# Stores of a feed-forward stage through GpSimd's transfer queue, and the next column's raw weight tiles requested at a column's start

## The chip, the core and the metric

The kernel runs on one core of a Trainium2 chip. Its engines are TensorE (PE, with weight loads shown as PEld), VectorE (DVE), ScalarE (ACT), GpSimd (POOL) and SyncE (SP, which only issues transfers here). Each engine works through its own list of instructions in the order in which the built program has them, and waits on semaphores where it needs another's result. The metric is the device time of one execution in microseconds.

## The reference

Two layers of a bidirectional encoder. Each has a mixer (gated linear attention in layer 0, spatial gating in layer 1) and a SwiGLU feed-forward block, with normalisations and conditioning around them. What the change touches lies in the feed-forward block, which occurs once in each layer:

```
a, bb = jnp.split(h @ ffn_w_in[i], 2, axis=-1)
y = (jax.nn.silu(a) * bb) @ ffn_w_out[i]
x = x + g2 * rms_norm(y, norm_g[i, 3])
```

`h` has 1024 features. There are 1024 tokens of one request, and 256 of another; the same weights serve both. `ffn_w_in` is 1024 x 5632 (2816 hidden features for `a`, 2816 for `bb`), `ffn_w_out` is 2816 x 1024. All in 32-bit floats.

## The kernel before

**Numbers.** A float32 operand is split into two parts that TensorE takes at full rate: a rounded high part (a cast on ACT, line 145) and the rest (a subtraction on DVE, line 146). Each product is then three matmuls: high by high, high by low, low by high.

**Token blocks.** The 1024 tokens are two blocks, A and B, of 512; the 256 tokens of the other request are block C.

**First feed-forward product, `ffn_in`.** It goes over 22 columns of 128 hidden features. The first two are done plainly. The other 20 (the loop `for j in range(NPL, NH)`) take blocks A and B together with the seven products of a Strassen-like scheme, so that four combinations of a column's weights are needed: `ua`, `us`, `ub`, `ut`. `ua` and `ub` are the raw weight tiles of the `a` half and the `bb` half, 128 x 1024 each (called A-tile and B-tile in the prediction). `us` and `ut` are made from both by four DVE operations (`sums`, lines 173 to 176: first the sum of the B-tile's halves, last the A-tile overwritten in place). Each of the four is split on ACT and DVE (lines 145, 146). The raw tiles come from a pool of three buffers (`rawp`). The loads are issued on SP by `raw` (lines 131, 134).

In the loop, one PSUM bank `a` collects several products in a row. It is read by DVE between them: line 1337 adds it to `c22`, and only when that has read it may TensorE start the next group, `seven(a, wb, 1, T[4], False)`. Line 1348 reads it once more for `gb`. Line 1341 finishes block C's column, which line 1264 (`store_c`) stores to `gdr`.

**Beside the columns.** Two generators run between the column's groups, by a credit that `tick` gives:

- `rights` (lines 1211 to 1231): for every two columns, it builds seven combinations of the products and stores them to `tdr`, 256 KB each (line 1213).
- `lefts` (lines 1234 to 1249): it prepares combinations of `ffn_w_out` for the second product. It works in 22 pieces for each layer. A piece loads two 256 KB halves into one buffer `y` (line 1240), does four DVE operations (lines 1242, 1243, 1245, 1246) in place, and stores 512 KB to `sdr` (line 1248). There is one buffer, so that the next piece's loads wait for the store to land.

**What sets the order.** The code is written in the order of the above, but the framework's scheduler orders each engine's instructions itself, by its own estimates. In the built program all 22 pieces of a layer stand in the first ten or eleven columns, two or three to a column; in an even column they stand otherwise than in an odd one. All transfers go through SP's queue, in the order that SP has them: an SP entry that waits holds up those behind it. GpSimd has 42 entries in the whole program, none of them within a layer's 20 columns.

Of the kernel before, what the change touches and what calls it, by code (L numbers as in the profile page):

```python
# [38 lines left out]
def encoder_kernel(  # L39
# [7 lines left out]
    nc = tc.nc  # L47
    pe, act, dve, pool, dma = nc.tensor, nc.scalar, nc.vector, nc.gpsimd, nc.sync.dma_start

    const = ctx.enter_context(tc.tile_pool(name="const", bufs=1))  # L50
    hp = ctx.enter_context(tc.tile_pool(name="hp", bufs=1))
    rawp = ctx.enter_context(tc.tile_pool(name="rawp", bufs=3))
# [6 lines left out]
    def nm(s):  # L59
        uid[0] += 1  # L60
        return f"{s}_{uid[0]}"
# [9 lines left out]
    def ps_ax():  # L71
        return psp.tile([128, 512], F32, tag="ax", bufs=3, name=nm("pax"))

    def ps_so():
        return psp.tile([128, 512], F32, tag="so", bufs=3, name=nm("pso"))
# [22 lines left out]
    src = {"A": (x_sample[0], 0), "B": (x_sample[0], 512), "C": (x_prompt[0], 0)}  # L98
# [15 lines left out]
    g_dr = [drp.tile([128, NH, 256], F32, name=nm("gdr")) for _ in range(2)]  # L114
    t_dr = [{o: drp.tile([128, NK, 512], F32, name=nm("tdr" + o)) for o in RUNS} for _ in range(2)]
    s_dr = [drp.tile([128, NK, 4, 512], F32, name=nm("sdr")) for _ in range(2)]


    class Units:
        def __init__(self):  # L120
            self.specs = []
            self.ready = []
            self.pos = 0
            self.n = 0
            self.spare = None
            self.pair = None

        def raw(self, src, shape):
            raw = rawp.tile([128, 1024], F32, tag="raw", name=nm("raw"))
# [19 lines left out]
        def load(self):  # L149
            key, src, shape = self.specs[self.pos]  # L150
            self.pos += 1
            n = 1024
            if key[0] == "ua":
                self.pair = [self.raw(x, 128) for x in src]
                w = self.pair[0]
            elif key[0] == "us":
                w = self.sums()
            elif key[0] == "ub":
                w = self.pair[1]
            elif key[0] == "ut":  # L160
                w = self.pair[0]
            else:
                w = self.raw(src, shape)
                if shape is not None:
                    n = src.shape[1] * src.shape[2]
            self.ready.append((key, *self.parts(w, key[0][0] == "u", n)))

        def sums(self):
            a, b = self.pair
            s = self.sum_tile()  # L170
            a1, a2, b1, b2 = a[:, 0:512], a[:, 512:1024], b[:, 0:512], b[:, 512:1024]
            s1, s2 = s[:, 0, :], s[:, 1, :]
            dve.tensor_add(s1, b1, b2)  # L173
            dve.tensor_sub(s2, s1, a1)
            dve.tensor_sub(a1, a1, b1)
            dve.tensor_sub(a2, a2, s2)
            return s.rearrange("p s c -> p (s c)")
# [5 lines left out]
        def next(self, key, ahead=2):  # L183
            self.ahead(1)
            k, hi, lo = self.ready.pop(0)
            assert k == key, (k, key)
            self.ahead(ahead)
            return hi, lo

    units = Units()  # L190
# [991 lines left out]
    def ffn_in(L, gens_in, fp, t_in):  # L1182
        td = t_dr[L]
# [26 lines left out]

        def rights(k, a, b, c, d):
            def put(o, t):
                dma(out=td[o][:, k, :], in_=t)

            yield 3.0
            for o, t in (("1", a), ("2", c), ("3", d)):
                put(o, t)
            x = bt.tile([128, 512], F32, tag="r", name=nm("x"))
            dve.tensor_sub(x, b, a)
            yield 1.4  # L1220
            dve.tensor_sub(b, d, b)
            yield 1.4
            put("5", x)
            dve.tensor_add(a, b, a)
            yield 1.4
            put("7", b)
            dve.tensor_sub(c, a, c)
            yield 1.4
            put("6", a)
            yield 1.4  # L1230
            put("4", c)


        def lefts():
            w = ffn_w_out[L].rearrange("(k t p) (h c) -> k p t h c", t=2, p=128, h=2)
            for k in range(NK):
                for c0 in (0, 256):
                    t = both[:, 2:4, :].rearrange("p i (u c) -> p (i u) c", u=2)
                    for i in range(2):
                        dma(out=t[:, 2 * i : 2 * i + 2, :], in_=w[k][:, i, :, c0 : c0 + 256])  # L1240
                    yield 12.0
                    dve.tensor_add(t[:, 3, :], t[:, 1, :], t[:, 3, :])
                    dve.tensor_sub(t[:, 1, :], t[:, 0, :], t[:, 1, :])
                    yield 1.0
                    dve.tensor_sub(t[:, 0, :], t[:, 3, :], t[:, 0, :])
                    dve.tensor_sub(t[:, 2, :], t[:, 2, :], t[:, 0, :])
                    yield 6.0
                    dma(out=s_dr[L][:, k, :, c0 : c0 + 256], in_=t)
                    yield 1.0

        def x_part(blk, h):
            return tuple(t[blk][:, 4 * h : 4 * h + 4, :] for t in (hhi, hlo))

        def seven(ps, w, half, x, start):
            hi, lo = w
            xh, xl = x
            for k in range(4):
                c = slice((4 * half + k) * 128, (4 * half + k + 1) * 128)
                for l, r in ((hi, xh), (hi, xl), (lo, xh)):
                    pe.matmul(ps, lhsT=l[:, c], rhs=r[:, k, :], start=start, stop=(k == 3 and l is lo), skip_group_check=True)  # L1260
                    start = False

        def store_c(j, s):
            dma(out=g_dr[L][:, j, :], in_=s)

        def plain(blk, j, w, part, s):
            n = BLK[blk]
# [12 lines left out]
        ua, ub = [], []  # L1280
        for ib, blk in enumerate(ORDER):
# [4 lines left out]
            for j in range(NPL):  # L1286
# [3 lines left out]
                if blk == "C":  # L1290
                    s = bt.tile([128, 256], F32, tag="accC", bufs=1, name=nm("gc"))
                else:
                    s = place[blk][:, j, :]
# [7 lines left out]
        both = ypart("A", 1)  # L1301
        units.sum_tile = lambda: both[:, 0:2, :]
        fill.push(lefts())
        for j in range(NPL, NH):
            last = j == NH - 1
            wa, ws, wb, wt = [units.next((u, L, j), 0) for u in ("ua", "us", "ub", "ut")]
            a, c = ps_so(), ps_ax()
            t1 = bt.tile([128, 512], F32, tag="t", name=nm("c11"))
            u2 = bt.tile([128, 512], F32, tag="r", name=nm("u2"))
            seven(a, wa, 0, x_part("B", 0), True)  # L1310
            act.copy(t1, a)
            tick(2.7, 0.7)
            seven(c, wa, 1, x_part("B", 1), True)
            dve.tensor_add(t1, t1, c)
            act.activation(t1, t1, AF.Silu)
            tick(2.7, 0.7)
            units.ahead(2)
            pc = ps_ax()[:, :256]
            mm3(pc, wa, "C")
            sc = bt.tile([128, 256], F32, tag="xk", bufs=3, name=nm("sc"))  # L1320
            act.activation(sc, pc, AF.Silu)
            tick(2.9, 0.7)
            seven(a, ws, 1, T[2], False)
            act.copy(u2, a)
            tick(2.7, 0.7)
            b = psp.tile([128, 512], F32, tag="mm", bufs=2, name=nm("pmm"))
            seven(b, ws, 0, x_part("A", 0), True)
            c22 = bt.tile([128, 512], F32, tag="sq", name=nm("c22"))
            act.copy(c22, b)
            tick(2.7, 0.7)  # L1330
            if not last:
                units.ahead(3)
            else:
                t_in(2, 2)
            vec.drain()
            seven(a, wt, 0, T[3], False)
            dve.tensor_add(c22, c22, a)  # L1337
            tick(2.7, 0.7)
            pc = ps_ax()[:, :256]
            mm3(pc, wb, "C")  # L1340
            dve.tensor_mul(sc, sc, pc)
            store_c(j, sc)
            tick(2.9, 0.7)
            if not last:
                units.ahead(4)
            seven(a, wb, 1, T[4], False)
            gb = t1 if j % 2 else bt.tile([128, 512], F32, tag="accB", bufs=1, name=nm("gb"))
            dve.tensor_mul(gb, t1, a)
            tick(2.7, 0.7)
            seven(b, wt, 1, x_part("A", 1), False)  # L1350
            t2 = bt.tile([128, 512], F32, tag="xk", bufs=3, name=nm("c12"))
            dve.tensor_add(t2, u2, b)
            act.activation(t2, t2, AF.Silu)
            ga = t2 if j % 2 else bt.tile([128, 512], F32, tag="accA", bufs=1, name=nm("ga"))
            dve.tensor_mul(ga, t2, c22)
            if j % 2:
                vec.push(rights(j // 2, *even, ga, gb))
            else:
                even = ga, gb
            tick(2.7, 0.7)  # L1360
# [378 lines left out]
```

## Time and profile before

| | |
|---|---|
| median of 3 runs | 2790.35 us (2790.24 to 2792.02) |
| the profiled execution's own time | 2790.62 us |
| its span, first to last instruction | 2788.9 us |
| mean granted TensorE clock | 0.991 |
| PE busy | 2714.6 us, 97% of the span |
| DVE busy | 1774.4 us, 64% |
| ACT busy | 1117.3 us, 40% |
| POOL busy | 36.1 us, 1% |
| transfers | 410.41 MB, all issued on SP but for instructions; engines of the queue busy 44.9% |

How to read it: PE is the engine to keep busy, and 74 us of the span it is not. The questions are where these lie, and what ended each. A row of the view of waits names the engine that waited, with the tile and line of its instruction, then what ended the wait, then the total in us, the number of waits, and the longest. A row of the timeline gives the start and the duration in us, the engine (with q for its sequencer), the line, the operation and the tiles, written first; in brackets stands the idle time before it. In these rows `y` is the buffer of `lefts` and also other tiles, `c` is `c11`, `c12` or `c22`, and `raw<-in_ffn_w_in_dram` is a raw weight tile.

Line 1337, once in each of the 20 columns, runs from 776.4 to 1262.6 us of the span in layer 0, and from 2003.5 to 2496.1 us in layer 1.

### The profile page before, as it was taken

The numbers are of one execution on the slowest core, as the hardware profiler recorded it, in microseconds if no ns is written. First come the engines' busy times: TensorE is split into PE (matmuls) and PEld (weight loads), VectorE is DVE, ScalarE is ACT, GpSimd is POOL, SyncE is SP. The second block draws the span as 40 slices with busy tenths as digits, with TensorE's granted clock in tenths as the row PEclk, the third lists the DMA queues.
The fourth block names the chain that finished last, engine by engine and source line by source line (L and its number), as shares of the span: only waits on it lengthen the run. The fifth ranks groups of instructions, "written<-read, shape, count | busy, mean of one in ns | idle before, by whom it ended". The sixth has DMA issues, their size and how long they took to land.

```text
span 2788.9 us, 36997 instructions
## 1 busy us (share of the span) xinstructions
PE 2714.6 (97%) x14164; PEld 2279.1 (82%) x14164; DVE 1774.4 (64%) x2781; ACT 1117.3 (40%) x1892; POOL 36.1 (1%) x48
## 2 busy tenths in 40 slices
PE   7999999999999999999999999999999999999998
PEld 4887888977888788888778888878878888888886
DVE  6762746587865654447778587676855644447576
ACT  5442434454632223324357354426422223234443
POOL 0001000000000000000000000000000000000000
PEclk9999999999999999999999999999999999999999
DMA  6224232156255542237777312454255532238676
GB/s 232 69 67 144 80 108 71 52 170 188 95 168 166 188 137 77 96 97 261 265 244 242 125 39 93 153 158 148 94 167 177 176 99 89 74 125 296 209 238 210
DMA packets 317542, 410.41 MB, mean 147 GB/s; under 512 B 21058, under 2 KB 194820, under 8 KB 317364
## 3 DMA queue, kind: packets, MB, share of 16 engines
q1 hardware_dynamic: 317364, 408.04, 44.9%
q8 instruction: 111, 1.82, 0.3%
q14 instruction: 67, 0.55, 0.1%
HBM read 304.65 MB, written 103.32 MB: 146 GB/s over the span
## 4 chain that ended last, share of the span: by engine, by line
PE 70%; DVE 12%; DMA 12%; issue 2%; ACT 2%; SPq 1%; POOL 0%; DVEq 0%; ACTq 0%; POOLq 0%
PE pso L1260 11%; PE pmm L1260 5%; PE pmm L322 4%; DMA y<-in_ffn_w_out_dram 3%; PE pax L1260 3%; PE pmm L309 2%; PE pmm L308 2%; PE pmm L307 2%; PE pax L307 2%; PE pax L308 2%; PE pso L1433 2%; PE pax L309 2%; PE pso L1434 2%; PE pso L1435 2%; DVE ulo L146 2%
## 5 line engine op out<-in xcount | busy, mean ns | idle before, releaser
L145 ACT CAST uhi<-raw 128x1024 fp32r<-128x1024 f32 (+1 forms) x299 | 307.2, 1030 | 648.7 <-issue 285.3
L146 DVE TENSOR_TENSOR ulo<-raw,uhi 128x1024 fp32r<-128x1024 f32 (+1 forms) x299 | 358.5, 1201 | 215.9 <-ACT uhi L145 214.6
L309 PE MATMUL pax<-hhiC,ulo 128*128 128x256 f32 x680 | 192.6, 283 | 0.0
L307 PE MATMUL pax<-hhiC,uhi 128*128 128x256 f32 x680 | 192.5, 283 | 0.0
L308 PE MATMUL pax<-hloC,uhi 128*128 128x256 f32 x680 | 192.4, 283 | 0.0
L1260 PE MATMUL pso<-t,uhi 128*128 128x512 f32 x428 | 149.8, 412 | 24.1 <-DVE c L1337 24.1
L1433 PE MATMUL pso<-uhi,hhiB 128*128 128x512 f32 x374 | 146.0, 391 | 0.9 <-DVE y L1416 0.5
L1434 PE MATMUL pso<-uhi,hloB 128*128 128x512 f32 x374 | 145.6, 389 | 0.0
L1435 PE MATMUL pso<-ulo,hhiB 128*128 128x512 f32 x374 | 145.6, 389 | 0.0
L307 PEld LDWEIGHTS pax<-hhiC,uhi 128*128 128x128 f32 x680 | 130.3, 192 | 3.8 <-ACT v L580 0.4
L308 PEld LDWEIGHTS pax<-hloC,uhi 128*128 128x128 f32 x680 | 130.2, 191 | 3.1
L309 PEld LDWEIGHTS pax<-hhiC,ulo 128*128 128x128 f32 x680 | 130.2, 191 | 1.7 <-issue 1.7
L371 DVE SCALAR_TENSOR_TENSOR aacc<-wada,sct,aacc 128x1024 f32<-128x1024 f32 x98 | 122.1, 1279 | 13.4 <-DMA wada<-in_w_ada_dram 13.3
L1382 ACT CAST hhiB<-tl 128x512 fp32r<-128x512 f32 x154 | 94.6, 619 | 89.1 <-DMA tl<-tdr 33.2
L1383 DVE TENSOR_TENSOR hloB<-tl,hhiB 128x512 fp32r<-128x512 f32 x154 | 106.0, 701 | 34.1 <-ACT hhiB L1382 34.0
L1260 PEld LDWEIGHTS pso<-t,uhi 128*128 128x128 f32 x428 | 81.4, 197 | 42.5 <-DVE c L1337 26.3
L1260 PE MATMUL pso<-y,uhi 128*128 128x512 f32 x324 | 109.2, 391 | 0.0
L173 DVE TENSOR_TENSOR y<-raw 128x512 f32<-128x512 f32 x40 | 27.6, 691 | 109.1 <-DMA raw<-in_ffn_w_in_dram 109.1
L1433 PE MATMUL pmm<-uhi,hhiB 128*128 128x512 f32 x242 | 94.7, 391 | 0.3 <-ACT y L1403 0.3
L1434 PE MATMUL pmm<-uhi,hloB 128*128 128x512 f32 x242 | 94.2, 389 | 0.0
L1435 PE MATMUL pmm<-ulo,hhiB 128*128 128x512 f32 x242 | 94.2, 389 | 0.0
L1433 PEld LDWEIGHTS pso<-uhi,hhiB 128*128 128x128 f32 x374 | 70.2, 188 | 18.6 <-DVE y L1416 1.4
(470 smaller groups left out, 7296.8 us busy)
## 6 DMA issues: line engine op xcount, KB each, us to landing
wada<-in_w_ada_dram SPq DMA_DIRECT2D x96, 512.0 KB
raw<-in_ffn_w_in_dram SPq DMA_DIRECT2D x88, 512.0 KB
tl<-tdr SPq DMA_DIRECT2D x154, 256.0 KB
raw<-in_ffn_w_out_dram SPq DMA_DIRECT2D x74, 512.0 KB
y<-in_ffn_w_out_dram SPq DMA_DIRECT2D x88, 256.0 KB
sdr<-y SPq DMA_DIRECT2D x44, 512.0 KB
raw<-sdr SPq DMA_DIRECT2D x40, 512.0 KB
tdr<-c SPq DMA_DIRECT2D x60, 256.0 KB
```

The costliest lines, as they stand in the source:

```text
L145: act.copy(hi[:, :n], raw[:, :n])
L146: dve.tensor_sub(lo[:, :n], raw[:, :n], hi[:, :n].bitcast(F32))
L307: pe.matmul(ps, lhsT=hi[:, c], rhs=hhi[blk][:, k, :], start=(k == 0), stop=False)
L308: pe.matmul(ps, lhsT=hi[:, c], rhs=hlo[blk][:, k, :], start=False, stop=False)
L309: pe.matmul(ps, lhsT=lo[:, c], rhs=hhi[blk][:, k, :], start=False, stop=(k == KD - 1))
L322: pe.matmul(ps, lhsT=l, rhs=r, start=(i == 0), stop=(i == 3 * KD - 1))
L371: dve.scalar_tensor_tensor(out=a, in0=ring[k % 2], scalar=sc, in1=a, op0=ALU.mult, op1=ALU.add)
L1260: pe.matmul(ps, lhsT=l[:, c], rhs=r[:, k, :], start=start, stop=(k == 3 and l is lo), skip_group_check=True)
L1383: dve.tensor_sub(lo, t, hi.bitcast(F32))
L1433: pe.matmul(ps, lhsT=th[:, t], rhs=hi[:, c], start=(k == 0), stop=False)
L1434: pe.matmul(ps, lhsT=tl[:, t], rhs=hi[:, c], start=False, stop=False)
L1435: pe.matmul(ps, lhsT=th[:, t], rhs=lo[:, c], start=False, stop=(k == NK - 1))
```

## The change

The three kinds of stores of `ffn_in` (to `tdr`, `sdr` and `gdr`) are issued by GpSimd and no longer by SP: 154 stores to `tdr`, 44 to `sdr` and 44 to `gdr`. And the raw tiles of the next column are requested when a column begins, by a method of their own, instead of with the next `ua`.

```diff
+    store = pool.dma_start
...
-                self.pair = [self.raw(x, 128) for x in src]
+                if self.coming is None:
+                    self.pairs_ahead()
+                self.pair, self.coming = self.coming, None
                 w = self.pair[0]
...
+        def pairs_ahead(self):
+            if self.coming is None:
+                key, src, shape = next((x for x in self.specs[self.pos - 1 :] if x[0][0] == "ua"), (None, None, None))
+                if key is not None:
+                    self.coming = [self.raw(x, 128) for x in src]
...
             def put(o, t):
-                dma(out=td[o][:, k, :], in_=t)
+                store(out=td[o][:, k, :], in_=t)
...
-                    dma(out=s_dr[L][:, k, :, c0 : c0 + 256], in_=t)
+                    store(out=s_dr[L][:, k, :, c0 : c0 + 256], in_=t)
...
         def store_c(j, s):
-            dma(out=g_dr[L][:, j, :], in_=s)
+            store(out=g_dr[L][:, j, :], in_=s)
...
             wa, ws, wb, wt = [units.next((u, L, j), 0) for u in ("ua", "us", "ub", "ut")]
+            if not last:
+                units.pairs_ahead()
```

What it does to the order of instructions: TensorE's order is the same, and DVE's and ACT's differ by exchanges of neighbours. SP's list is shorter by the stores, and GpSimd's is longer by them. In the changed kernel the line numbers are 1 to 11 higher.

On SP, in layer 0, within one odd column of the time when `lefts` runs. `y` is the buffer of `lefts`, `raw` with a number a raw weight tile (8436 is a B-tile, 8628 the A-tile of the column after). Before:

```order
L1240 DMA y_6838<-in_ffn_w_out_dram 128x2x256 x2
L1213 DMA tdr_36_123<-ga_8203 128x512
L1248 DMA sdr_137<-y_6838 128x4x256
L1240 DMA y_6838<-in_ffn_w_out_dram 128x2x256
L134 DMA raw_8436<-in_ffn_w_in_dram 128x8x128
L1213 DMA tdr_41_128<-x_8414 128x512
L1240 DMA y_6838<-in_ffn_w_out_dram 128x2x256
L134 DMA raw_8628<-in_ffn_w_in_dram 128x8x128
L1248 DMA sdr_137<-y_6838 128x4x256
L1264 DMA gdr_121<-sc_8281 128x256
```

After, the same place (8396 is that B-tile, 8597 that A-tile):

```order
L1249 DMA y_6838<-in_ffn_w_out_dram 128x2x256 x4
L135 DMA raw_8396<-in_ffn_w_in_dram 128x8x128
L1249 DMA y_6838<-in_ffn_w_out_dram 128x2x256 x2
L135 DMA raw_8597<-in_ffn_w_in_dram 128x8x128
L1249 DMA y_6838<-in_ffn_w_out_dram 128x2x256 x4
```

The stores are gone from between the loads. The B-tile's load now stands ahead of both `y` loads of its piece, where it stood between them; the A-tile's load stands behind them as it did.

On GpSimd, which had nothing there before, the same stretch now reads (the first five rows belong to the odd column, the rest to the even column after it):

```order
L1257 DMA sdr_137<-y_6838 128x4x256
L1222 DMA tdr_36_123<-ga_8203 128x512
L1257 DMA sdr_137<-y_6838 128x4x256
L1222 DMA tdr_41_128<-x_8418 128x512
L1257 DMA sdr_137<-y_6838 128x4x256
L1273 DMA gdr_121<-sc_8281 128x256
L1222 DMA tdr_42_129<-c_1380_8213 128x512
L1222 DMA tdr_38_125<-gb_8186 128x512
L1222 DMA tdr_37_124<-ga_8203 128x512
L1222 DMA tdr_40_127<-c_1394_8390 128x512
L1257 DMA sdr_137<-y_6838 128x4x256
```

All stores of a layer are now one list of their own, in the order in which DVE finishes their data. Four stores to `tdr` and one to `gdr` stand ahead of the last store to `sdr` in this piece.

More of the change, by code (lines that the diff above doesn't have):

```diff
@@ L125, in __init__ @@
             self.spare = None
-            self.pair = None
+            self.pair = self.coming = None
         def raw(self, src, shape):
```

## The prediction

> **What bounds the kernel now.** I read the page first, then the waits of TensorE, then three stretches of equal work side by side, then the timelines of VectorE and SyncE in the stretch that loses time.
>
> ```profile
> PE 2714.6 (97%) x14164; PEld 2279.1 (82%) x14164; DVE 1774.4 (64%) x2781; ACT 1117.3 (40%) x1892; POOL 36.1 (1%) x48
> PE pso L1260 <- DVE c L1337: 24.1, 11, 4.6
> ```
>
> TensorE is the bound, and GpSimd is free. The largest wait of TensorE in the whole program, 24.1 us in 11 places, is for line 1337, in the stage that the change touches. The next view gives the columns from one line 1337 to another: eight of layer 0 and nine of layer 1, with the pieces of `lefts` in them, and two later ones, with no pieces left. (Columns: length, then busy time of PE, PEld, DVE, ACT, POOL, then granted clock, DMA share, GB/s.)
>
> ```profile
> 776.36:989.27 212.91, 203.51 (x1056) 174.49 (x1055) 127.75 (x209) 58.36 (x80) 0.00 (x0) 0.98 0.54 176
> 2003.46:2246.96 243.50, 229.59 (x1193) 196.63 (x1191) 142.04 (x231) 65.39 (x90) 0.00 (x0) 0.99 0.52 169
> 1088.47:1138.19 49.72, 49.72 (x265) 42.91 (x264) 24.31 (x34) 14.84 (x20) 0.00 (x0) 1.00 0.26 85
> ```
>
> A free column takes 49.72 / 2 = 24.86 us. Eight take 198.9, so layer 0 loses 14.0 us; nine take 223.7, so layer 1 loses 19.8. These 33.8 us are all that better transfers in this stage could bring, and only these 17 columns, 8.5 pairs, are near enough to the limit to lose more.
>
> Why they lose it is seen in one pair, an even column and the odd one behind it. First the even one on VectorE, then on SyncE:
>
> ```profile
> 917.26 0.69 DVE L1348 TENSOR_TENSOR c<-c,pso 128x512 f32<-128x512 f32 x1 [3.13 <-PE pso L1260]
> ...
> 923.87 0.41 DVE L1242 TENSOR_TENSOR y<-y 128x256 f32<-128x256 f32 x1
> ...
> 932.80 0.42 DVE L1242 TENSOR_TENSOR y<-y 128x256 f32<-128x256 f32 x1 [2.26 <-DMA y<-in_ffn_w_out_dram]
> ...
> 935.20 0.69 DVE L173 TENSOR_TENSOR y<-raw 128x512 f32<-128x512 f32 x1 [0.60 <-DMA raw<-in_ffn_w_in_dram]
> ```
>
> ```profile
> 918.07 0.55 SPq L1213 DMA_DIRECT2D tdr<-c  x1
> ...
> 925.69 0.37 SPq L1248 DMA_DIRECT2D sdr<-y  x1
> ...
> 928.66 1.20 SPq L1240 DMA_DIRECT2D y<-in_ffn_w_out_dram  x2
> ...
> 934.64 0.37 SPq L1248 DMA_DIRECT2D sdr<-y  x1
> ```
>
> Then the odd one, likewise:
>
> ```profile
> 942.62 0.42 DVE L1242 TENSOR_TENSOR y<-y 128x256 f32<-128x256 f32 x1 [2.80 <-DMA y<-in_ffn_w_out_dram]
> ...
> 944.00 0.43 DVE L1246 TENSOR_TENSOR y<-y 128x256 f32<-128x256 f32 x1
> ...
> 951.42 0.42 DVE L1242 TENSOR_TENSOR y<-y 128x256 f32<-128x256 f32 x1 [1.60 <-DMA y<-in_ffn_w_out_dram]
> ...
> 955.00 1.23 DVE L146 TENSOR_TENSOR ulo<-raw,uhi 128x1024 fp32r<-128x1024 f32 x1 [1.30 <-ACT uhi L145]
> ...
> 962.26 0.69 DVE L173 TENSOR_TENSOR y<-raw 128x512 f32<-128x512 f32 x1 [5.43 <-DMA raw<-in_ffn_w_in_dram]
> ...
> 964.73 0.42 DVE L1242 TENSOR_TENSOR y<-y 128x256 f32<-128x256 f32 x1
> 965.07 0.68 DVE L1337 TENSOR_TENSOR c<-c,pso 128x512 f32<-128x512 f32 x1
> ```
>
> ```profile
> 944.46 0.37 SPq L1248 DMA_DIRECT2D sdr<-y  x1
> 947.38 1.20 SPq L1240 DMA_DIRECT2D y<-in_ffn_w_out_dram  x2
> ...
> 953.73 0.37 SPq L1248 DMA_DIRECT2D sdr<-y  x1
> 956.64 0.55 SPq L1240 DMA_DIRECT2D y<-in_ffn_w_out_dram  x1
> 957.23 0.60 SPq L134 DMA_DIRECT2D raw<-in_ffn_w_in_dram  x1
> 957.93 1.31 SPq L1213 DMA_DIRECT2D tdr<-x  x1
> 959.28 0.55 SPq L1240 DMA_DIRECT2D y<-in_ffn_w_out_dram  x1
> ```
>
> The pieces are a loop of their own: store, wait until it has landed (944.46 to 947.38, 2.92 us), load, wait, four operations, store. VectorE takes its list in order, so each of its waits for `y` holds up line 1337, and TensorE behind it. Five pieces fall on the pair. The first (923.87) begins with no idle time. The next three (932.80, 942.62, 951.42) each wait for their load: here the store is on the path. The fifth (964.73) again has no idle time: it stands behind line 173, which waited 5.43 us for a raw tile. So the chain of the pair runs from 917.26, where VectorE waits for TensorE, through three round trips of a store, to 965.07.
>
> **The change part by part.** *Raw tiles asked for early.* The B-tile of the next column needs the buffer that line 146 frees at 955.00 + 1.23 = 956.23, and it is issued at 957.23. In the free columns, with nothing else on the queue, the same three rows follow each other:
>
> ```profile
> 1105.68 1.23 DVE L146 TENSOR_TENSOR ulo<-raw,uhi 128x1024 fp32r<-128x1024 f32 x1 [3.13 <-ACT uhi L145]
> ...
> 1111.30 0.69 DVE L173 TENSOR_TENSOR y<-raw 128x512 f32<-128x512 f32 x1 [3.78 <-DMA raw<-in_ffn_w_in_dram]
> ```
>
> ```profile
> 1106.94 0.38 SPq L134 DMA_DIRECT2D raw<-in_ffn_w_in_dram  x1
> ```
>
> The load goes out as soon as the buffer is free (1105.68 + 1.23 = 1106.91), and VectorE still waits 3.78 us. It is the three buffers that set this, not the moment of asking, and the order shown above has the same releases. Worth: zero, bounded by 0 and the 1.0 us from 956.23 to 957.23, in which the B-tile's load stands behind a `y` load. Of this I count 0.6 us, since the new order puts the B-tile ahead (0.59 us between 956.64 and 957.23); that is a saving per pair.
>
> *Stores off SyncE.* SyncE gets rid of 242 issues. Where they delayed a load, as at 957.93 (1.31 us before the second `y` load at 959.28), the piece had no idle time to lose at 964.73. I count nothing for it, and what covers it is the raw tile's wait of 5.43; if that shrinks, the 1.31 us count too.
>
> *Stores on GpSimd.* The trace shows no store issued there, so its extra time X over SyncE's, from VectorE's last subtraction to landing, is unknown. The nearest rows are an issue on SyncE, and GpSimd's own instructions (the columns of the latter: busy us, mean ns, idle time before):
>
> ```profile
> L1248 SPq DMA_DIRECT2D sdr<-y x44: 359/366/377, 773.0 to 2238.6; - x44
> L406 POOL TENSOR_TENSOR wada<-wada 2x512 f32<-2x512 f32 x6 | 9.9, 1649 | 1.8 <-DMA wada<-in_norm_g_dram 1.6
> L406 POOL TENSOR_TENSOR adar<-adar 2x512 f32<-2x512 f32 x2 | 4.2, 2108 | 1.1 <-DMA adar<-in_norm_g_dram 1.1
> L392 POOL MEMSET wada<- 64x512 f32 x7 | 3.6, 521 | 1969.8 <-DMA tl<-tdr 1334.0 <-DVE aacc L371 364.4 <-DMA wada<-in_w_ada_dram 241.8
> ```
>
> A store costs SyncE 0.37 us. GpSimd's ordinary two-input instruction takes 1.65 us. If a store takes it about that long, X = 1.65 - 0.37 = 1.28, say 1.3. Below, X could be -0.37, if the issue costs GpSimd nothing; above, a fill and the slowest two-input instruction together, 0.52 + 2.11 - 0.37 = 2.26. I take 1.3, because a store to `sdr` writes its list of 512 rows by program, which is nearer to an instruction that works through data than to a mere issue. The Trainium skill, "DMA: Bandwidth & Descriptors", section Specifications, gives a first-byte latency of about 1 us for transfers issued on GpSimd and 0.6 us for SyncE's; by that X would be an estimated 0.4 us and the change -5.1 us in all (only the saving of 0.6 us a pair would be left), and no run here shows it yet.
>
> *The sum.* On the pair's chain stand three stores: 3X = 3.9 us. Against it stand the 1.3 us that VectorE idles for ACT at 955.00, which take up delay, and the 0.6 us saved: 3X - 1.9 = 2.0 us for a pair. The fifth store's 1.3 us hide behind the raw tile's wait, and the first one's behind the operations from 917.26 to 923.87. In the even column the delay before line 173 (0.60 idle) is absorbed in part, which only moves where it is seen. For 8.5 pairs: +17.0 us. On GpSimd only other stores are queued behind a store, and nobody waits soon for those to `tdr` and `gdr`. On SyncE the `y` loads wait X longer, and behind them stand the next A-tile and the loads after it; the A-tile has a whole column's time. The bytes moved are the same. On the profiled execution's 2790.62 us this makes 2807.6, so 2808 (that execution is 0.3 us over the median of 2790.35; I make no correction).
>
> **The rivals.** About 0.2%, 5.6 us, is what a measurement of this kernel can tell from no change.
>
> *No change (X below 0.87).* Up to X = 0.43, 3X stays within the 1.3 us of slack, and only the saving is left: 8.5 x 0.6 = 5.1 us, 2785.5. At X = 0.87 the pair loses 0.7 us, 6.0 us in all, 2796.6: the other edge. For it: SyncE's 0.37 us shows that an issue need not be dear. Against it: GpSimd's rows above are all over 0.5 us. The skill's two latencies, quoted above, belong to this case.
>
> *Faster: the shared queue was what made the raw tile late.* At 962.26 the raw tile cost 5.43 us of idle time, in the free column 3.78 us. If the load, ahead of `y` and with no `tdr` beside it, takes only the latter, a pair gains 1.65 us more. With X within the slack (0.43) that makes 8.5 x (0.6 + 1.65) = 19.1 us, 2771.5. It needs X under 0.96 to show (3X - 1.3 = 1.6, which leaves 0.65 of the 2.25 us a pair, 5.5 us in all); above X = 1.18 the loss outweighs it. Against it: other loads still run beside it, and `y` comes later into the same time.
>
> *GpSimd's list itself is the bound.* Between 918.07, when SyncE could issue the first of four stores to `tdr`, and 925.69 lie 7.6 us; at up to 1.9 us a store, GpSimd is through in time. At 3.0 us it would be 12.0 - 7.6 = 4.4 us late with the store to `sdr`, and X would be 2.63: a pair loses 3 x 2.63 - 1.9 + 4.4 = 10.4 us, in all 88 us, 2879. Against it: no instruction of GpSimd shown takes 3 us.
>
> **How the numbers follow.** Slower by X of 0.87 to 2.26: chance 0.55; its own range is 2796 to 8.5 x (6.78 - 1.9) = +41.5, 2832. GpSimd's list as the bound: 0.05. No change: 0.24. Faster: 0.16. So slower by over 0.2% has 0.60, within 0.2% 0.24, faster 0.16. Time: that of the likeliest, 2808. The range goes up to 2832, which leaves out the 0.05 and a little more, and down to 2780, half way into the faster case, which leaves out about 0.1 (below X = 0.43 with the raw tile's full gain).
>
> **What would show it.** In the changed kernel's trace, from the end of a piece's last subtraction on VectorE to its `y` loads about 2.92 + 1.3 = 4.2 us. Line 1242's idle times in the pairs grow by about 1.3 us each where they exist, TensorE's wait for the `c22` addition (line 1337) grows from 24.1 to about 40 us, and the free columns stay at 24.86 us. Line 173's wait in the free columns stays at 3.8; if it vanishes, the early asking did work. I am wrong if X is far from 1.3; if the scheduler's new order lets VectorE meet a wait earlier than before; or if the store's data, later by X, collide with the raw tile's load.

## The result and the profile after

The changed kernel takes 2817.17 us in the median (2815.89 to 2819.38), the kernel before 2790.3 us on the same chip. The ratio is 1.0096, with a 95% interval of 1.0082 to 1.0109: slower by about 27 us. The forecast was 2808, with a range of 2780 to 2832.

The profiled execution has a span of 2815.9 us against 2788.9. First the page's line of busy times, then the view of waits of TensorE and of VectorE (line 1337 of before is 1348 now, 1242 is 1251, 173 is 182, 1248 is 1257):

```profile
PE 2728.2 (97%) x14164; PEld 2286.5 (81%) x14164; DVE 1774.2 (63%) x2781; ACT 1115.9 (40%) x1892; POOL 176.1 (6%) x290
```

```profile
PE pso L1269 <- DVE c L1348: 36.3, 15, 5.7
...
PE pmm L1444 <- ACT y L1414: 2.3, 1, 2.3
```

```profile
DVE y L1251 <- DMA y<-in_ffn_w_out_dram: 129.3, 30, 5.9
DVE y L182 <- DMA raw<-in_ffn_w_in_dram: 98.9, 33, 6.5
```

The same two waits of VectorE in the kernel before:

```profile
DVE y L173 <- DMA raw<-in_ffn_w_in_dram: 109.1, 32, 5.9
DVE y L1242 <- DMA y<-in_ffn_w_out_dram: 96.4, 30, 5.5
```

And GpSimd's row for the `sdr` stores (count, shortest, median and longest in ns):

```profile
L1257 POOL DMA_DIRECT2D sdr<-y x44: 759/768/771, 774.1 to 2273.2; - x44
```

GpSimd is busy for 6% of the span, so its list is no bound. TensorE's wait for the `c22` addition has grown by 12.2 us, from 24.1. VectorE waits 32.9 us more for `y`, in as many places as before, and 10.2 us less for raw tiles. TensorE's wait is less than half of the 27 us. The rest stands in the first line: the same 14164 matmuls keep TensorE busy 13.6 us longer.

Where this lies is seen in three pairs of stretches, cut at the `c22` additions: from a layer's first to its last (19 columns; length, then PE's busy time, the granted clock with 1.00 for full speed, the mean busy share of the transfers' engines, GB/s). Before, then after:

```profile
776.36:1262.57 486.21, 476.81 (x2500) 0.99 0.41 131
2003.46:2496.09 492.63, 477.98 (x2492) 0.99 0.40 129
sum 978.84, PE 954.79; mean PE 477.39
```

```profile
776.99:1280.39 503.40, 483.20 (x2500) 0.98 0.39 127
2024.27:2522.90 498.63, 482.16 (x2500) 0.98 0.39 127
sum 1002.03, PE 965.36; mean PE 482.68
```

The two layers' columns give 1002.03 - 978.84 = 23.2 us of the 27.0. PE is idle 12.6 us more in them and busy 10.6 us more. Between the layers the stretch grows from 2003.46 - 1262.57 = 740.9 to 743.9 us; ahead of the first column and behind the last one 0.8 us are left.

The busy time is the clock. The traces' records of the granted clock have, within these columns, 5 stretches of 3.41 us at half speed before and 11 after; six more, at half of 3.41 us each, make 10.2 of the 10.6 us. The stretch behind one of the longest waits of TensorE, in the changed kernel, in steps of 3 us:

```profile
859.00:862.00 3.00, 0.00 (x0) 1.00 0.44 136
862.00:865.00 3.00, 1.10 (x3) 0.54 0.24 70
865.00:868.00 3.00, 3.00 (x9) 0.50 0.73 234
868.00:871.00 3.00, 3.00 (x13) 0.83 0.44 148
871.00:874.00 3.00, 3.00 (x15) 1.00 0.78 283
```

TensorE idles, and then works at half its clock for some 5 us: 9 matmuls in 3 us, where 15 go at full clock. This wait is paid once as idle time and again as slow work.

What a piece of `lefts` does now is seen in one odd column, first on VectorE, then on GpSimd, then on SyncE:

```profile
964.93 0.42 DVE L1255 TENSOR_TENSOR y<-y 128x256 f32<-128x256 f32 x1
965.27 1.22 DVE L147 TENSOR_TENSOR ulo<-raw,uhi 128x1024 fp32r<-128x1024 f32 x1
...
972.12 0.69 DVE L182 TENSOR_TENSOR y<-raw 128x512 f32<-128x512 f32 x1 [5.03 <-DMA raw<-in_ffn_w_in_dram]
...
974.93 0.68 DVE L1348 TENSOR_TENSOR c<-c,pso 128x512 f32<-128x512 f32 x1
```

```profile
965.81 0.76 POOL L1257 DMA_DIRECT2D sdr<-y  x1 [5.88 <-DVE y L1255]
```

```profile
966.52 0.37 SPq L135 DMA_DIRECT2D raw<-in_ffn_w_in_dram  x1
970.32 1.20 SPq L1249 DMA_DIRECT2D y<-in_ffn_w_out_dram  x2
```

The last subtraction ends at 965.35. GpSimd issues the store 0.46 us later (SyncE, in the kernel before, did so after 0.03 us in the median), and the next `y` loads go out at 970.32, 4.97 us after the subtraction. Over the 42 store-to-load steps of both layers the median from subtraction to load is 4.02 us, against 2.97 before: 0.43 us of the difference lie ahead of the issue, and 0.55 us behind it (3.49 against 2.94; each of these is a median of its own). So X is 1.05 us. The second thing to see: the B-tile's load leaves at 966.52, as soon as its buffer is free (965.27 + 1.22 = 966.49), but 0.71 us behind the store, and is there only at 972.12. In the prediction's pair (957.23) it left 0.59 us behind a `y` load, with the store landed.

### The profile page after: what moved, and what is told of

It is laid out like the page before. It is cut to its first block, busy times and chain, and to the rows that moved or that the text cites. A ratio compares the mean times of both kernels' runs of the same rounds, so it can differ in the third digit from the quotient of the medians.

```text
span 2815.9 us, 37177 instructions
## 1 busy us (share of the span) xinstructions
PE 2728.2 (97%) x14164; PEld 2286.5 (81%) x14164; DVE 1774.2 (63%) x2781; ACT 1115.9 (40%) x1892; POOL 176.1 (6%) x290
## 4 chain that ended last, share of the span: by engine, by line
PE 62%; DMA 13%; DVE 11%; issue 10%; ACT 2%; POOL 1%; SPq 1%; POOLq 0%; DVEq 0%; ACTq 0%
PE pso L1269 9%; PE pmm L1269 4%; PE pmm L331 4%; DMA y<-in_ffn_w_out_dram 4%; DMA sdr<-y 3%; PE pso L1444 2%; PE pso L1445 2%; PE pso L1446 2%; PE pax L1269 2%; PE pmm L316 2%; PE pmm L318 2%; PE pmm L317 2%; DMA wada<-in_w_ada_dram 2%; PE pmm L1444 2%; PE pmm L1445 2%
## 5 line engine op out<-in xcount | busy, mean ns | idle before, releaser
L1269 PE MATMUL pso<-t,uhi 128*128 128x512 f32 x428 | 155.2, 425 | 36.4 <-DVE c L1348 36.3
L1251 DVE TENSOR_TENSOR y<-y 128x256 f32<-128x256 f32 x44 | 18.6, 423 | 129.3 <-DMA y<-in_ffn_w_out_dram 129.3
```

## The experiments

All ratios are to the kernel before, run in the same turns (medians 2789.64 to 2791.01 us).

**Which part of the change costs.** The first theory, *round trip*: only the store to `sdr` matters, as it alone is in a loop. Its rivals: *order* (the early asking moved the loads) and *list* (the 198 small stores on GpSimd).

Stores on GpSimd, no early asking:

```diff
-            if not last:
-                units.pairs_ahead()
```

> All three kinds of stores on GpSimd, the raw tiles asked for as before. Round trip (the store to sdr takes about 1.05 us longer from VectorE's last subtraction to the next y load, 4.02 against 2.97 us in the medians of the two traces, and that is the whole cause): as the changed kernel, 2812 to 2820 us, with 34 to 38 us of TensorE waiting for the c22 addition. Order (the early asking put the B-tile ahead of y, and that made y late): near the kernel before, 2787 to 2796 us, with 22 to 28 us of that wait.

Early asking, stores on SyncE:

```diff
-    store = pool.dma_start
+    store = dma
```

> The raw tiles asked for early, all stores on SyncE. Round trip: as the kernel before, 2785 to 2796 us, waits for the c22 addition of 22 to 28 us. Order: as the changed kernel, 2810 to 2820 us. If the early asking saves the 0.6 us a pair that the prediction counted, 2785 us and not more.

The change with the `sdr` stores alone back on SyncE:

```diff
-                    store(out=s_dr[L][:, k, :, c0 : c0 + 256], in_=t)
+                    dma(out=s_dr[L][:, k, :, c0 : c0 + 256], in_=t)
```

> The changed kernel, but the 44 stores to sdr back on SyncE; the 198 to tdr and gdr stay on GpSimd, the early asking stays. Round trip: as the kernel before or a little better, 2780 to 2795 us, since only the sdr store is in a loop. List (the many small stores on GpSimd, by their landing or by what they hold up, are the cost): 2805 to 2817 us.

The change with the `tdr` and `gdr` stores back on SyncE:

```diff
-                store(out=td[o][:, k, :], in_=t)
+                dma(out=td[o][:, k, :], in_=t)
...
-            store(out=g_dr[L][:, j, :], in_=s)
+            dma(out=g_dr[L][:, j, :], in_=s)
```

> The changed kernel, but the stores to tdr and gdr back on SyncE; only the 44 to sdr on GpSimd, the early asking stays. Round trip: as the changed kernel, 2808 to 2820 us, and the time from a piece's last subtraction to its next load stays at 4.0 us in the median. List: near the kernel before, 2787 to 2797 us, with that time nearer to 3.5 us, as no store to tdr stands ahead on GpSimd.

Measured (columns: the two 19-column stretches in sum, cut as above; between: the stretch from one to the other, in the profiled executions):

| kernel | median us | ratio (95%) | columns | PE busy in them | between |
|---|---|---|---|---|---|
| before | 2790.3 | 1 | 978.8 | 954.8 | 740.9 |
| changed | 2817.17 | 1.0096 (1.0082 to 1.0109) | 1002.0 | 965.4 | 743.9 |
| stores on GpSimd, no early asking | 2810.51 | 1.0069 (1.0053 to 1.0086) | 996.5 | 960.5 | 746.8 |
| early asking only | 2788.35 | 0.9994 (0.9984 to 1.0004) | 977.9 | 957.2 | 743.9 |
| `sdr` back on SyncE | 2793.17 | 1.0017 (1.0004 to 1.0029) | 977.8 | 956.2 | 744.6 |
| only `sdr` on GpSimd | 2807.64 | 1.0060 (1.0044 to 1.0075) | 997.7 | 963.4 | 740.0 |

The stores to `sdr`, with the early asking, make the columns 18.9 us longer; without them the columns are as before, early asking and all. *Order* falls: the early asking by itself moves nothing that can be measured. *List* falls as the main cause. Two medians lie just under the ranges of *round trip*: 2810.51 (2812 to 2820) and 2807.64 (2808 to 2820). The profiled execution of the early asking alone was the slowest of its 12, 2797.7 us; its columns are as before all the same. The page's rows of transfers show the same store on each queue (KB each, median us from issue to landing), with `sdr` back on SyncE:

```profile
sdr<-y SPq DMA_DIRECT2D x44, 512.0 KB, 2.9
```

and in the changed kernel:

```profile
sdr<-y POOLq DMA_DIRECT2D x44, 512.0 KB, 3.4
```

With only `sdr` on GpSimd, subtraction to load is 3.82 us in the median, not the 4.0 expected: with the small stores on GpSimd too it is some 0.2 us longer. The `tdr` and `gdr` stores cost about 0.2%, 3 to 5 us, and not in the columns. In the three of these profiled executions that have them on GpSimd, TensorE waits 2.3 to 3.5 us once at the start of the second product (line 1444 in the changed kernel, shown above) for a copy on ACT, which stands behind casts that wait for loads of `sdr` and `tdr`; in the other three that wait is 0.3 us or none. That this wait is their whole cost is not shown: the stretch between the columns is as long (743.9 us) in the execution with the early asking only. The early asking beside the stores (2817 against 2810 us) may cost some 0.3%; the two were not run in the same turns, the intervals just meet, and this is left open.

**Whether the place of the wait or the loop of pieces decides.** TensorE's last two groups of a column, exchanged, give the `c22` addition 2.7 us more time. The edit, made in the kernel before and in the changed one:

```diff
+            seven(b, wt, 1, x_part("A", 1), False)
             if not last:
                 units.ahead(4)
             seven(a, wb, 1, T[4], False)
...
-            seven(b, wt, 1, x_part("A", 1), False)
```

> The kernel before, with TensorE's groups seven(b, wt) and seven(a, wb) exchanged, so that 2.7 us more work stand between the c22 addition's data and the group that needs it. If lateness of that addition by 2 to 7 us is what TensorE loses in the stage, most of its 24.1 us of waits go, and with them most of the 10.6 us in which the columns run longer without a wait (the clock at 0.50 after a wait): 2755 to 2768 us. If the loop of the pieces, not the place of the wait, sets the pace (five pieces a pair at 9.9 us each are 49.5 us, a pair of columns 49.7), VectorE falls behind further instead and it stays at 2780 to 2792.

> The same exchange in the changed kernel. If only the place of the wait matters, the 2.7 us absorb most of the longer round trip as well: 2760 to 2775 us, within 8 us of the exchanged kernel before. If the loop of pieces sets the pace (five at 10.9 us are 54.5 us against 49.7 of a pair), it stays slower than that by most of the 27 us: 2785 to 2812.

Measured: 2785.28 us (0.9977, 0.9965 to 0.9990) and 2808.09 us (1.0063, 1.0048 to 1.0077). The waits for the addition fell (24.1 to 10.8 us, and 36.3 to 15.6), while new ones came for ACT's copy to `u2` (4.0 and 9.2 us). The columns fell to 966.9 and 983.2 us; but the two kernels stay 16.3 us apart in them, and 22.8 in all. So the extra store time isn't absorbed by moving the wait once, which fits a loop of pieces that VectorE is bound to. Of the gain of 11.9 us in the columns of the kernel before, the times show only 5 to 6 us. The profiled execution has a stretch of 752.0 us between the layers, but it was the slowest of 12 (2798.57 us), so that it doesn't show where the rest went in the others. The forecasts that the place of the wait decides, 2755 to 2768 and 2760 to 2775, were wrong; both times lie in the ranges given for the loop of pieces.

**Taking the store off the path.** Each piece's loads are tied to the newest `c22`, by a copy of four numbers on GpSimd into the buffer, which the loads then overwrite. The scheduler can no longer put five pieces on a pair:

```diff
                     t = both[:, 2:4, :].rearrange("p i (u c) -> p (i u) c", u=2)
+                    if mark:
+                        pool.tensor_copy(t[0:1, :, 0:1], mark[0][0:1, 0:4].rearrange("p (i c) -> p i c", c=1))
...
+        mark = []
         fill.push(lefts())
...
             dve.tensor_add(c22, c22, a)
+            mark[:] = [c22]
```

> The kernel before, with each piece's loads tied to the newest c22 (a copy of four numbers on GpSimd into the buffer, overwritten by the load), so that 22 pieces spread over 18 columns, one or two to a column, and not 5 to a pair. Round trip: with some 20 us to a piece the store is off the path, TensorE's waits for the c22 addition fall below 8 us and the granted clock in the stage comes to 1.00: 2752 to 2765 us. If something else in the stage (raw tiles, VectorE's amount of work) makes the addition late, the losses spread over more columns and it stays at 2780 to 2795.

> The same tie in the changed kernel. Round trip: the store's extra 1.05 us has room, so that it comes within 4 us of the paced kernel before, 2752 to 2767 us, though each store still takes 4.0 us. If GpSimd's stores cost by anything else than the loop of the pieces (TensorE's clock, transfers that collide), 15 to 27 us stay between the two: 2770 to 2790.

Measured: 2784.34 us (0.9980, 0.9965 to 0.9994) and 2798.0 us (1.0034, 1.0021 to 1.0048). Both gained less than expected, and they stay 13.7 us apart. The columns told why: in the order that was built, four columns of each layer still had two pieces, both tied to one `c22`, so that they ran back to back. At the first, second and fourth of these TensorE waited 1.4 to 3.0 us in the kernel before and 3.0 to 4.8 in the changed one, at the third 1.0 to 1.5, and in the other columns 1.2 at most.

So the tie was moved to the newer of `c22` and `ga`, half a column apart, and the credit that a piece takes was raised:

```diff
-                    yield 12.0
+                    yield 13.5
...
             dve.tensor_mul(ga, t2, c22)
+            mark[:] = [ga]
```

> The kernel before, with each piece's loads tied to the newest c22 or ga, whichever is later, and 21.5 us of credit to a piece in place of 20, so that no two pieces are tied to the same event. In the paced kernels TensorE waited for the c22 addition only in the columns that had two pieces tied to one c22 (the third, seventh, eleventh, sixteenth). Round trip: these waits go, less than 6 us of them are left in the two layers together, and both layers' 19 columns come to 473.7 + 2 each, 949 to 955 us in sum against 982.0 before: 2750 to 2768 us. Otherwise (a wait for y costs in any column): as the paced kernel before, 2778 to 2788.

> The same in the changed kernel. Round trip: the 19 columns of both layers come within 6 us of the spread kernel before, since nothing waits for a store; only the 3 to 6 us that the stores to tdr and gdr cost at the start of the second product are left: 2754 to 2774 us. If a store on GpSimd costs in another way, 14 us stay between the two, as between the paced ones.

Measured: 2768.39 us (0.9917, 0.9903 to 0.9930) and 2785.32 us (0.9982, 0.9973 to 0.9992). With all stores on SyncE this beats both kernels: 956.2 us of columns against 978.8, and the wait for the addition at a third. Time, columns and waits each lie just outside what was expected of them (2768, 955 and 6 us):

```profile
PE pso L1262 <- DVE c L1340: 8.3, 6, 2.0
```

No wait for it is longer than 2.0 us, and one stretch of 3.41 us at half clock is left in the columns. But the second half of the expectation failed: with the stores on GpSimd the columns take 970.0 us, 13.8 more, and the stretch between them 745.9 us against 740.5. So the changed kernel stays slower when the pieces are spread. The two differ in the small stores and the early asking too, which were not separated here as they were above. The next views show what else differs. In the spread kernel before, on VectorE and SyncE:

```profile
1071.82 0.43 DVE L1248 TENSOR_TENSOR y<-y 128x256 f32<-128x256 f32 x1
...
1077.64 0.69 DVE L173 TENSOR_TENSOR y<-raw 128x512 f32<-128x512 f32 x1 [4.26 <-DMA raw<-in_ffn_w_in_dram]
```

```profile
1072.27 0.38 SPq L1250 DMA_DIRECT2D sdr<-y  x1
1073.41 0.38 SPq L134 DMA_DIRECT2D raw<-in_ffn_w_in_dram  x1
```

In the spread changed kernel, on VectorE, GpSimd and SyncE:

```profile
1076.37 0.43 DVE L1257 TENSOR_TENSOR y<-y 128x256 f32<-128x256 f32 x1
...
1083.35 0.69 DVE L182 TENSOR_TENSOR y<-raw 128x512 f32<-128x512 f32 x1 [5.42 <-DMA raw<-in_ffn_w_in_dram]
```

```profile
1077.57 0.76 POOL L1259 DMA_DIRECT2D sdr<-y  x1 [2.76 <-DVE y L1257]
```

```profile
1077.96 0.37 SPq L135 DMA_DIRECT2D raw<-in_ffn_w_in_dram  x1
```

The B-tile's load leaves when line 146 (147 in the changed kernel) has freed its buffer, 1.2 us behind the subtraction in both. SyncE's store was then 1.14 us ahead of it, GpSimd's 0.39 us; from the load's issue to the addition that reads it pass 4.23 and 5.39 us. Over the 18 such loads of each kernel the medians are 4.42 and 5.38. The store and the load move 512 KB each, and run at the same time. This suggests a second cost of a late store: *collision*. About 1 us at 18 loads makes 17 us of VectorE's time, the size of the 13.8; that it is the cause was left to two more runs.

**Late, or in another queue.** Two last kernels on the spread ones. A copy on GpSimd between the last subtraction and SyncE's store, to make that store as late as GpSimd's:

```diff
+                    pool.tensor_copy(t[0:1, 3, 0:4], t[0:1, 3, 0:4])
                     dma(out=s_dr[L][:, k, :, c0 : c0 + 256], in_=t)
```

> The spread kernel before (all stores on SyncE), with a copy of four numbers on GpSimd between a piece's last subtraction and its store to sdr, so that SyncE issues the store some 0.8 us later, which is about as late as GpSimd issued it (0.77 us after the last subtraction's end at 1077.57, against some 0.03 on SyncE). In the spread changed kernel the raw B-tile's load, when a store had been issued less than 3 us ahead of it, took 4.98 us in the median from its issue to the addition that reads it (19 of them), in the spread kernel before 3.41 (18). Lateness (the store's data still run when the load is issued): loads of 4.5 to 5.2 us here too, the 19 columns of both layers 965 to 974 us in sum, and 2774 to 2784 us. Queue (a store in another queue takes turns with the load, one in the same queue does not): loads of 3.3 to 3.9 us, 957 to 962 us, 2764 to 2773.

Measured: 2769.88 us (0.9927, 0.9913 to 0.9941), columns 956.0. The loads' times in this expectation, 4.98 and 3.41 us, were taken from a later record of SyncE's queue than the issue; from the issue they are the 5.38 and 4.42 above, and here 4.43. But the edit failed its purpose: the copy touched only a part of `y` that earlier operations use, so that it ran beside the last subtraction (in most pieces it ended 0.04 us behind it), and the store still went out 0.07 us behind the subtraction (0.03 without the copy). It says nothing of *lateness* against *queue*, and only repeats the result of the spread kernel before.

And the store held back until the raw tile is in:

```diff
+                    for _ in range(3):
+                        pool.tensor_copy(t, t)
                     store(out=s_dr[L][:, k, :, c0 : c0 + 256], in_=t)
```

> The spread changed kernel, with three copies of y onto itself on GpSimd ahead of each store to sdr, so that the store goes out 4 to 6 us later, when the raw B-tile has landed. Collision (the store's data, which come beside the raw tile's load, are what is left of the cost in the stage): the loads come back to 3.4 to 3.7 us, the columns of both layers fall from 972 to 958 to 964 us in sum, and with the 4 to 6 us at the start of the second product the time is 2768 to 2778 us. Round trip (each microsecond of the store still counts): slower than the spread changed kernel, 2787 to 2810.

Measured: 2820.75 us (1.0108, 1.0091 to 1.0125), columns 1004.5, TensorE's wait for the addition 42.0 us. The three copies took 4.5 us, and 0.5 us more passed before the store. Of the 31 raw loads that VectorE waited for, 18 now had no store within 4 us ahead of them and none close behind, against 12 in the spread changed kernel, and took 3.9 us; 6 still met a store, half a microsecond ahead, and took 5.2 to 6.2. So the collision goes where the store is out of the way. But the round trip is some 4.3 us longer than in the spread changed kernel (5.04 against 0.73 us from the subtraction to the store), and where two pieces are half a column apart that is too long again: TensorE waited up to 7.6 us there. This cost far more than the collision had. The *round trip* expectation came true, and the two costs of the spread changed kernel could not be separated by this run.

What the other eleven traces with that order of TensorE show on lateness, sorted by how long a store to `sdr` was issued ahead of a raw load that VectorE then waited for, with the median time from the load's issue to the addition (number of loads):

| store ahead by (us) | stores on SyncE | stores on GpSimd |
|---|---|---|
| 0.3 to 0.6 | - | 5.38 (24) |
| 0.6 to 1.0 | - | 5.56 (9) |
| 1.0 to 1.3 | 4.53 (50) | 4.81 (9) |
| none within 4 | 4.20 (106) | 4.01 (89) |

In the one row of a near store that both queues have, they are 0.3 us apart; between a store 1.1 us and one half a microsecond ahead lie 0.6 to 0.9. This speaks for *lateness* as the larger part. But each of the two rows in the middle has 9 loads on GpSimd, and the row of 0.6 to 1.0 does not lie between its neighbours, as lateness alone would have it. It is read from the traces, and no run made for it shows it.

## Why the prediction was right, and where its sum was not

The sign and the mechanism held: the price of a `sdr` store on GpSimd is on the path, and the kernel with only these stores on GpSimd (and the early asking, which alone costs nothing) is slower by 0.60%, some 17 us. That 2808 came near is in part luck: X was 0.25 us too high, for a wrong reason, which is 6.4 us over three stores in 8.5 pairs, and this stood in for a part of the slow clock that no term had. Point by point:

- *X.* Taken 1.3 us; measured 1.05 (4.02 - 2.97), or 0.85 with no other stores on GpSimd. The reason given was wrong, however: the issue takes GpSimd 0.77 us, and not the 1.65 of an ordinary instruction. The time is lost in two other places: 0.43 us more pass from the subtraction's end until GpSimd's issue begins, and 0.55 us more from the issue to the next load. The Trainium skill, "DMA: Bandwidth & Descriptors", section Specifications, has 1 us against 0.6 us to the first byte; the estimate of 0.4 us from it is near the second of these parts, and does not hold the first. What GpSimd does in the 0.43 us no row shows.
- *Per pair.* With the measured X, 3X - 1.9 = 1.25 us, and 8.5 pairs make 10.6 us. TensorE's idle time in the columns grew by 12.6 us. Without the 0.6 us of saving, which did not come (below), the same sum gives 15.7. With only `sdr` on GpSimd (X of 0.85) the two are 5.5 and 10.6, and the idle time grew by 10.2. So the term had the right size, but its parts are not confirmed one by one.
- *The step that failed* is the sum itself: it took a microsecond of waiting as a microsecond of time. Half clock after the waits added another 10.6 us of PE busy time in the columns (11 stretches of 3.41 us, where there were 5), and no term stood for it, though the row of layer 0 in the prediction shows a clock of 0.98. The wait of 24.1 us and the loss of 33.8 us in the prediction's own numbers differ by 9.7 us; that gap was the sign of it.
- *The 0.6 us a pair saved* by the B-tile ahead of `y`: its load did leave at once (966.49 to 966.52), but then ran beside the store, as the last of the prediction's warnings said, and took 5.60 us. With the stores on SyncE the early asking gives 0.9994, nothing measurable. The term should have been zero.
- *"Nobody waits soon" for the stores to `tdr` and `gdr`*: true in the columns (977.8 us with them on GpSimd, 978.8 before), not at the layer's end, where TensorE now waits 2.3 to 3.5 us.
- *What was to be seen.* Subtraction to load 4.2 us: 4.02. Line 1242's idle times, 1.3 us more each: 32.9 us more in 30 places, 1.1 us each. TensorE's wait about 40 us: 36.3. Line 173's wait in the free columns about 3.8 us: 3.94 and 3.35 at 1103.75 and 1128.69. The free columns' length, 24.86 us: the next stretch.

```profile
1081.22:1131.16 49.94, 49.94 (x267) 43.13 (x266) 24.31 (x34) 14.77 (x20) 4.87 (x9) 1.00 0.26 85
```

Two free columns at 24.97 us each, with PE busy throughout: the stores that remain there on GpSimd let TensorE wait for nothing.

- *The rivals.* No change needed X under 0.87, which the single-part kernel's 0.85 reaches; it was slower all the same: PE's busy time in its columns is 8.6 us longer, from the clock, and the 0.6 us of saving that this bound counts on did not come. Of the faster case a part came true: VectorE's wait for raw tiles fell by 10.2 us, but its wait for `y` grew by 32.9. GpSimd's list as the bound is out, at 0.77 and 0.54 us an issue.

In sum, of the 27.0 us between the two traces 12.6 are the idle time that the forecast's 17.0 stood for, 10.6 are slow clock, 3.0 lie between the layers' columns, and 0.8 elsewhere. What share the collision has in the 12.6 was not separated in the kernel as changed. It is hardly a large one: only 7 of the 33 raw loads that VectorE waited for had a store less than 3 us ahead of them, against 5 of 32 before, and these waits are shorter in sum.

## What to carry to other kernels

A transfer inside a loop through one buffer (store, landing, load) can cost its latency at each turn, as it did here with the transfers' engines half idle. Before changing its queue, ask whether the turns can be spread, so that it is off the path: here that gave 0.8%, where no choice of a queue gained anything. And price a wait of the bounding engine with what follows it: the clock after the wait, and the next transfer that a late store meets.

## What the runs showed of the hardware

**The clock after a wait.** In the twelve profiled kernels without the exchanged groups, every column of the two layers was taken with the idle time of TensorE ahead of it and its excess over 24.93 us. The clock drops after waits well under 3.4 us:

| TensorE idle ahead (us) | columns | of these longer by over 1 us | mean excess |
|---|---|---|---|
| 0 to 1 | 353 | 2 | 0.08 |
| 1 to 2 | 35 | 2 | 0.26 |
| 2 to 2.6 | 15 | 10 | 1.20 |
| 2.6 to 3 | 17 | 13 | 1.51 |
| 3 to 3.5 | 19 | 18 | 1.77 |
| over 3.5 | 17 | 17 | 2.04 |

A usual excess is 1.65 to 1.7 us, as 3.41 us at half clock make it. The records of the granted clock show more. All stretches at half clock in the columns of these twelve traces last 3.41 us or twice that, and in each trace they begin on one grid of 3.41 us steps. What decides is how long TensorE was idle within the step just before. Where that step ran at full clock, the next was at half clock in none of the 3286 cases with less than 1.75 us of idle time, in 2 of 7 between 1.75 and 1.9, and in all 58 with more. Behind a step at half clock, 0.8 us of idle time or more kept it there (14 cases), and 0.5 or less did not (60). So a wait of 2 to 3.4 us costs the clock if enough of it falls into one step, which is why the rows in the middle of the table are mixed, and the usual price is half of 3.41 us. The Trainium skill, "TensorE: Matmul & The Clock Gate", section What's actually happening, tells of a free-running window of 3413 ns; an idle one halves the clock, and the section Why this matters for your kernels asks for no idle gaps over some 3 us. The length of the steps agrees; the limit is lower in these traces, where some 1.9 us of idle time in one step of 3.41 us were enough. The matmuls' ends are modelled in the trace, so that the limit may be off by some tenths.

**GpSimd as an issuer.** A store of 512 rows took its list 0.77 us, one of 128 rows 0.54; SyncE's were 0.37 and 0.33. For the stores to `sdr`, its issue began 0.43 us later behind the data than SyncE's, and the load that waited for the landing came another 0.55 us later.
